# Second block of a two-block transformer: two depthwise-convolution tiles move to ScalarE and GpSimd, two are summed in PSUM, and three more weight blocks are split

## The chip, the cores and the metric

The kernel runs on one core of one Trainium2 chip. The metric is the device time of one execution in microseconds (us). The engines are PE (TensorE, matmuls), DVE (VectorE), ACT (ScalarE), POOL (GpSimd) and SP (SyncE, which issues the loads of weights).

## The reference, cut to what matters

Two transformer blocks run one after the other on 256 tokens of width 1024. The change lies in the second block, whose mixer is half attention (8 heads of 64) and half a gated depthwise convolution over 512 channels with 31 taps:

```python
def conformer_conv(a, g, w_dw, b_dw, ln_g, ln_b):
    u = a * sigmoid(g)
    u = conv_general_dilated(u, w_dw[:, None, :], padding=((30, 0),), feature_group_count=512) + b_dw
    un = (u - mean(u)) * rsqrt(var(u) + 1e-5) * ln_g + ln_b      # over the 512 channels
    return silu(un)

u = rms_norm(h, mix_norm_g)
q, k, v, glu_a, glu_g = split(u @ w_in)
mixed = concat([attention(q, k, v), conformer_conv(glu_a, glu_g, ...)])
h = h + mixed @ w_out
u = rms_norm(h, ffn_norm_g)
h = h + (silu(u @ w_gate) * (u @ w_up)) @ w_down
return rms_norm(h, final_norm_g)
```

## The kernel before, in words

All weights pass through one `Stream` in blocks of 128 partitions x 2048 floats. SP loads a block into one of three raw buffers (`wraw`, L86), so block b waits until block b-3 is done with its buffer. Most blocks are then split: ACT rounds the block to `wh` (L103), DVE subtracts to get the rest `wl` (L104), and PE multiplies with three passes (`mm3`). Three pairs of split buffers rotate in the second block, and a fourth is added for `w_out`. Blocks listed in `NATIVE2` are not split: PE takes the raw fp32 block as it is, and the raw buffer is free only when its matmuls are done.

In the second block `w_in` has ten blocks. Blocks 0 to 3 give the four channel tiles of the convolution (128 channels each, gate and value), 4 and 5 give q, 6 and 7 give k, 8 and 9 give v. `convs` and `proj_cols` are the projections with the result in columns. For each channel tile `ct`, ACT makes the sigmoid `ga`, DVE multiplies to `ug` (L1298), and the convolution is a start (ACT, `cv` = scale times `ug` plus bias, L1310) followed by 30 shifted multiply-adds on DVE, each over 226 to 255 tokens and each on the result of the one before (L1314).

Attention runs in four `STEPS` of four heads by 128 tokens. `scores` makes the logits (PE, `lg`), the row maximum with the bias strip (DVE, `z`, L492), the exponential (ACT, L496), the reciprocal (DVE, L498) and the product with it (ACT, L501); `values` transposes and multiplies with v and splits the result into `oT`. The v projections of blocks 8 and 9 (`proj_tok`, group `pj`) lie behind the scores of steps 0 and 1 and share one PSUM bank, so block 9 waits for the ACT copy of block 8's result. Behind the attention come the layer norm of the convolution (`pmu`, `pvr`, `prs`), its silu, and `w_out` in eight parts of 12 matmuls (`Mix.part`, L196 `acc`), then the feed-forward part.

Each engine takes its instructions in the order in which a scheduler wrote them down when the kernel was built; an instruction that waits holds up all behind it on its engine. `tc.high_priority` and `tc.issue_after` bend that order.

Of the kernel before, what the change touches and what calls it, by code (L numbers as in the profile page):

```python
# [10 lines left out]
F32 = mybir.dt.float32  # L11
# [4 lines left out]
AF = mybir.ActivationFunctionType  # L16
ALU = mybir.AluOpType
AX = mybir.AxisListType

P = 128  # L20
D = 1024
T = 256
# [5 lines left out]
NE = 8  # L28
R_RAW = 3
N_SPLIT = 3  # L30
NATIVE2 = (0, 1, 4, 5, 6, 7)


class Buffers:
# [109 lines left out]
def tile_model(ctx, tc, io, out):  # L144
    nc = tc.nc
# [7 lines left out]
    def ffn_order(w1, w3, w2, n, lag=1):  # L153
        r = []
        for j in range(n):
            r += [w1[j], w3[j]]
            if j >= lag:
                r.append(w2[j - lag])
        return r + [w2[j] for j in range(n - lag, n)]
# [8 lines left out]
    for i in range(len(steps_) + 1):  # L168
        if i < len(steps_):
            e, j = steps_[i]  # L170
            moe_order += [io[n][e][j][kh] for n in ("w1_m", "w3_m") for kh in range(2)]
        if i:
            e, j = steps_[i - 1]
# [5 lines left out]
    order += ffn_order(io["w1_2"], io["w3_2"], io["w2_2"], NF)  # L179
    ws = Stream(tc, rawp, wp, order, native=[second + i for i in NATIVE2])  # L180

# [4 lines left out]
    def bank(group, name):  # L186

        i = groups[group][turns[group] % len(groups[group])]
        turns[group] += 1
        return ps.tile([P, 512], F32, tag="bank%d" % i, name=name)  # L190
# [4 lines left out]
    def mm(o, l, r, start, stop):  # L195
        return nc.tensor.matmul(o, l, r, start=start, stop=stop, skip_group_check=True)  # L196

    def mm3(o, lh, ll, rh, rl, start, stop):
        mm(o, lh, rh, start, False)
        mm(o, lh, rl, False, False)  # L200
        return mm(o, ll, rh, False, stop)
# [5 lines left out]
    def tok(tt):  # L207
        return slice(tt * P, (tt + 1) * P)

    def half(nh):  # L210
        return slice(nh * 512, (nh + 1) * 512)
# [53 lines left out]
    def new_xT():  # L265
        h = xp.tile([P, 8, T], F32R, tag="b8", name="xTh")
        l = xp.tile([P, 8, T], F32R, tag="b8", name="xTl")
        return h, l
# [6 lines left out]
    def take8():  # L275
        return [w if w is None else w.rearrange("p (k n) -> p k n", k=8) for w in ws.take()]
# [4 lines left out]
    def proj_cols(xT, full=None, group="mm"):  # L281

        wh, wl = take8()
        o = bank(group, "pc")
        for ct in range(2):
            for k in range(8):
                oc = o[:, ct * 256:(ct + 1) * 256]
                if wl is None:
                    mm(oc, wh[:, k, tok(ct)], full[:, k, :], k == 0, k == 7)
                else:  # L290
                    mm3(oc, wh[:, k, tok(ct)], wl[:, k, tok(ct)], xT[0][:, k, :], xT[1][:, k, :], k == 0, k == 7)
        return o.rearrange("p (c t) -> p c t", c=2)
# [283 lines left out]
    xT = new_xT()  # L576
# [9 lines left out]
    with tc.tile_pool(name="l0", bufs=1) as lp:  # L586
# [6 lines left out]
        qT = lp.tile([P, 4, T], F32, tag="qT", name="qT")  # L593
        kT = lp.tile([P, 4, T], F32, tag="kT", name="kT")
        vb = lp.tile([P, 2, 512], F32, tag="vb", name="vb")
        with tc.tile_pool(name="gla", bufs=1) as gp:
# [23 lines left out]
            for i in range(2):  # L620
                o = proj_cols(xT)
# [11 lines left out]
            for tt in range(2):  # L633
# [3 lines left out]
                for q in range(2):  # L637
# [5 lines left out]
                    for j in range(2):  # L643
                        rl = g2([P, 2, 256], "rl")
                        nc.scalar.activation(rl[:, :, :S], pis[j][:, :, :S], AF.Relu)
                        for i in range(2):
# [3 lines left out]
                                                           op0=ALU.mult, op1=ALU.add)  # L650
                            first = False
                for r in range(8):
# [4 lines left out]
                                               op0=ALU.not_equal, op1=ALU.max)  # L657
# [76 lines left out]
            for tt in range(2):  # L734
# [13 lines left out]
                for h in range(4):  # L748
                    nc.vector.scalar_tensor_tensor(o_s[:, h, :], o_s[:, h, :], rs[:, h:h + 1], sg[:, tt, tok(h)],
                                                   op0=ALU.mult, op1=ALU.mult)  # L750
# [9 lines left out]
        with tc.tile_pool(name="t0", bufs=1) as tp, tc.tile_pool(name="t0w", bufs=2) as wo:  # L760
# [25 lines left out]
            xT = xT2  # L786
# [3 lines left out]
    with tc.tile_pool(name="f0", bufs=2) as fp, tc.tile_pool(name="f0r", bufs=4) as fr, tc.tile_pool(name="f0w", bufs=1) as fw:  # L790
# [13 lines left out]
        x, xT = xn, xT2  # L804
# [62 lines left out]
    with tc.tile_pool(name="l1", bufs=1) as lp:  # L867
# [6 lines left out]
        with tc.tile_pool(name="fox", bufs=1) as gp:  # L874
# [41 lines left out]
            qT = gp.tile([P, 4, T], F32, tag="qT", name="qT")  # L916
# [30 lines left out]
        with tc.tile_pool(name="t1", bufs=1) as tp, tc.tile_pool(name="t1w", bufs=1) as wo:  # L947
# [5 lines left out]
            copied, logits, xTf = [], [], []  # L953
# [47 lines left out]
    with tc.tile_pool(name="moer", bufs=4) as mr, tc.tile_pool(name="moe2", bufs=2) as m2:  # L1001
# [229 lines left out]
        xT = new_xT()  # L1231
        xTf = xp.tile([P, 8, T], F32, tag="b8", name="xTf")
# [46 lines left out]
    with tc.tile_pool(name="s1", bufs=1) as lp:  # L1279
        def t2(shape, name):  # L1280
            return lp.tile(shape, F32, tag="t2", name=name, bufs=6)

        cw = load_const(lp, "conv_w")
        cpar = load_const(lp, "conv_p")
        strip = load_strip(lp, rows[2])
        c512 = lp.tile([P, P], F32, tag="c512", name="c512")
        nc.gpsimd.memset(c512, 1.0 / 512.0)
        ones = lp.tile([P, P], F32, tag="ones", name="ones")
        nc.gpsimd.memset(ones, 1.0)
        oT = new_oT()  # L1290
        ug = lp.tile([P, 4, T], F32, tag="ug", name="ug")
        ga = lp.tile([P, 4, T], F32, tag="ga", name="ga")
        cv = lp.tile([P, 4, T], F32, tag="cv", name="cv")
        ws.first = True
        for ct in range(4):
            o = convs[ct] if ct < 1 else proj_cols(xT, xTf)
            nc.scalar.activation(ga[:, ct, :], o[:, 0, :], AF.Sigmoid)
            nc.vector.tensor_tensor(ug[:, ct, :], ga[:, ct, :], o[:, 1, :], op=ALU.mult)  # L1298
        qT = lp.tile([P, 4, T], F32, tag="qT", name="qT")
        kT = lp.tile([P, 4, T], F32, tag="kT", name="kT")  # L1300
        for i in range(2):
            nc.scalar.activation(qT[:, 2 * i:2 * i + 2, :], proj_cols(xT, xTf), AF.Copy, scale=0.125)
        for i in range(2):
            nc.scalar.activation(kT[:, 2 * i:2 * i + 2, :], proj_cols(xT, xTf), AF.Copy)
        v = lp.tile([P, 2, 512], F32, tag="v", name="v")
        scores, values = attention(t2, t2, qT, kT, v, lambda h: strip[:, h, :], None, oT, 0, on_act=True)

        def conv(ct):

            nc.scalar.activation(cv[:, ct, :], ug[:, ct, :], AF.Identity, bias=cpar[:, 0, ct:ct + 1],  # L1310
                                 scale=cw[:, ct, 30:31])
            for j in range(30):
                back = 30 - j
                nc.vector.scalar_tensor_tensor(cv[:, ct, back:], ug[:, ct, :T - back], cw[:, ct, j:j + 1],  # L1314
                                               cv[:, ct, back:], op0=ALU.mult, op1=ALU.add)

        for i, step in enumerate(STEPS):
            conv(i)
            scores(*step)
            if i < 2:  # L1320
                nc.scalar.activation(v[:, :, i * 256:(i + 1) * 256], proj_tok(xT, group="pj"), AF.Copy)
            if i:
                values(*STEPS[i - 1])
        with tc.tile_pool(name="t2", bufs=1) as tp, tc.tile_pool(name="t2w", bufs=1) as wo:
            ffng = times32(bcast(tp, io["ffn_g"], "ffng"))
            ws.wider(4, wo, 1)
            xn = xp.tile([P, 2, D], F32, tag="b8", name="h1")
            xT = new_xT()

            def finish(tt, acc):  # L1330
                for nh in range(2):
                    nc.vector.tensor_tensor(xn[:, tt, half(nh)], x[:, tt, half(nh)], acc[nh], op=ALU.add)
                u = tp.tile([P, D], F32, tag="u", name="u", bufs=2)
                rms_tile(xn[:, tt], ffng, u)
                transpose_tile(u, "acc%d" % tt, parts_of(xT, tt))

            mix = Mix(oT, finish)

            pmu = bank("pj", "pmu")
            for ct in range(4):  # L1340
                mm(pmu[:, :T], c512, cv[:, ct, :], ct == 0, ct == 3)
            nc.vector.tensor_tensor(cv, cv, pmu[:, None, :T].to_broadcast([P, 4, T]), op=ALU.subtract)
            nc.scalar.activation(ga, cv, AF.Square)
            values(*STEPS[3])
            mix.part(0, 0)
            pvr = bank("pj", "pvr")
            for tt in range(2):
                for ct in range(4):
                    mm(pvr[:, tt:tt + 1], ga[:, ct, tok(tt)], c512[:, 0:1], ct == 0, ct == 3)
            vr = sp.tile([P, 2], F32, tag="vr", name="vr")  # L1350
            nc.vector.tensor_copy(vr, pvr[:, 0:2])
            rs = rstd_of(vr, 1e-5, n=2)
            mix.part(0, 1)
            dg = lp.tile([P, 2, P], F32, tag="dg", name="dg")
            prs = bank("pj", "prs")
            for tt in range(2):
                nc.vector.tensor_scalar(dg[:, tt, :], ident, rs[:, tt:tt + 1], None, op0=ALU.mult)
                mm(prs[:, tok(tt)], ones, dg[:, tt, :], True, True)
            nc.vector.tensor_tensor(cv, cv, prs[:, None, :T].to_broadcast([P, 4, T]), op=ALU.mult)
            for ct in range(4):  # L1360
                nc.scalar.activation(cv[:, ct, :], cv[:, ct, :], AF.Silu, bias=cpar[:, 2, ct:ct + 1],
                                     scale=cpar[:, 1, ct:ct + 1])
                split_to(oT[0][:, 4 + ct, :], oT[1][:, 4 + ct, :], cv[:, ct, :])
            ws.first = False
            for part in ((1, 0), (1, 1), (0, 2), (0, 3), (1, 2), (1, 3)):
                mix.part(*part)
            x = xn

    with tc.tile_pool(name="f2", bufs=2) as fp, tc.tile_pool(name="f2r", bufs=4) as fr, tc.tile_pool(name="f2w", bufs=1) as fw:
        fing = times32(bcast(fp, io["fin_g"], "fing"))  # L1370

        o = xp.tile([P, 2, D], F32, tag="b8", name="o")
# [158 lines left out]
```

## Time and profile before

| what | value |
|---|---|
| median of 3 runs | 1822.85 us (1820.8 to 1822.95) |
| the profiled execution, its own time | 1823.05 us |
| its span in the trace | 1821.3 us |
| PE, DVE, ACT, POOL busy, share of the span | 97%, 74%, 60%, 5% |

The span is what the trace covers; the 1.75 us around it are part of the measured time. The rows further below are from this one execution. Times in rows are us from the start of the span. A row of a busy time does not tell whether the engine was the one waited for; that is read from the waits and from the order.

### The profile page before, as it was taken

Reading aid. Unit: us, or ns where it says so; the run is one execution under the profiler, and the core shown is the slowest. Engines: PE = TensorE matmul, PEld = TensorE weight load, DVE = VectorE, ACT = ScalarE, POOL = GpSimd, SP = SyncE. Lnnn points to the kernel's source line nnn. Section 1 sums busy time; section 2 is a strip of 40 time slices with the busy share of each in tenths; the row PEclk is TensorE's granted clock in tenths of the full one; section 3 lists DMA queues with packets and bytes.
Section 4 is the critical chain, followed back from the end, with each engine's and each line's share of the span. In section 5 each row is a group of like instructions: output and inputs, shape, how many; then the busy total and the mean of one; then the engine's idle time right before and its main releaser. Section 6 shows DMA issues by size and latency. Waiting matters only on the chain. (4 is left out here: it accounts for less than half of the span.)

```text
span 1821.3 us, 24157 instructions
## 1 busy us (share of the span) xinstructions
PE 1772.5 (97%) x9687; PEld 1495.8 (82%) x9687; DVE 1341.7 (74%) x1370; ACT 1096.1 (60%) x1017; POOL 97.0 (5%) x136
## 2 busy tenths in 40 slices
PE   8999999999999999999999999999999989899998
PEld 7797999888678888888788787887887859789997
DVE  6956544546678888888888888888888978854443
ACT  5454434445567777777777777777777752564332
POOL 1101100010010000000000000000001021010000
PEclk9999999999999999999999999999999999899999
DMA  8453985265489999999999999999999914546530
GB/s 301 162 188 117 394 322 186 70 219 175 148 332 417 370 377 376 373 357 368 381 358 371 383 357 372 377 365 370 372 363 386 397 62 158 203 148 252 187 119 24
DMA packets 75415, 512.45 MB, mean 281 GB/s; under 512 B 8572, under 2 KB 8725, under 8 KB 17312
## 3 DMA queue, kind: packets, MB, share of 16 engines
q1 hardware_dynamic: 66240, 476.15, 69.0%
q0 software_dynamic: 8768, 34.18, 5.0%
q8 instruction: 77, 1.26, 0.3%
q10 hardware_dynamic: 288, 0.52, 0.1%
q14 instruction: 42, 0.34, 0.1%
HBM read 495.57 MB, written 19.96 MB: 283 GB/s over the span
## 5 line engine op out<-in xcount | busy, mean ns | idle before, releaser
L104 DVE TENSOR_TENSOR wl<-wraw,wh 128x2048 fp32r<-128x2048 f32 (+1 forms) x446 | 1012.1, 2287 | 291.7 <-ACT wh L103 290.4
L103 ACT ACTIVATE wh<-wraw 128x2048 fp32r<-128x2048 f32 (+1 forms) x446 | 851.9, 1913 | 458.0 <-issue 128.6
L196 PE MATMUL hh<-wl,eTh 128*128 128x512 f32 x896 | 355.9, 397 | 3.2 <-DVE wl L104 3.2
L196 PE MATMUL hh<-wh,eTh 128*128 128x512 f32 x896 | 355.1, 396 | 0.2 <-ACT eTh L204 0.2
L196 PE MATMUL hh<-wh,eTl 128*128 128x512 f32 x896 | 353.3, 394 | 0.0
L196 PE MATMUL pc<-xTh,wh 128*128 128x256 f32 x944 | 269.4, 285 | 1.4 <-ACT xTh L204 1.4
L196 PE MATMUL pc<-xTl,wh 128*128 128x256 f32 x944 | 268.6, 284 | 1.0 <-DVE xTl L205 1.0
L196 PE MATMUL pc<-xTh,wl 128*128 128x256 f32 x944 | 268.6, 285 | 0.0
L196 PEld LDWEIGHTS hh<-wl,eTh 128*128 128x128 f32 x896 | 168.8, 188 | 45.9 <-DVE wl L104 7.6
L196 PEld LDWEIGHTS hh<-wh,eTh 128*128 128x128 f32 x896 | 168.8, 188 | 39.0 <-ACT eTh L204 0.4
L196 PEld LDWEIGHTS hh<-wh,eTl 128*128 128x128 f32 x896 | 168.8, 188 | 38.0
L196 PEld LDWEIGHTS pc<-xTh,wh 128*128 128x128 f32 x944 | 182.1, 193 | 3.3 <-ACT xTh L204 1.6
L196 PEld LDWEIGHTS pc<-xTl,wh 128*128 128x128 f32 x944 | 182.0, 193 | 2.1 <-DVE xTl L205 1.2
L196 PEld LDWEIGHTS pc<-xTh,wl 128*128 128x128 f32 x944 | 182.2, 193 | 0.4 <-issue 0.2
L196 PE MATMUL acc<-wl,mah 128*128 128x512 f32 x448 | 180.8, 404 | 0.0
L196 PE MATMUL acc<-wh,mal 128*128 128x512 f32 x448 | 176.7, 395 | 0.3 <-DVE mal L205 0.3
L196 PE MATMUL acc<-wh,mah 128*128 128x512 f32 x448 | 163.6, 395 | 0.5 <-ACT mah L204 0.5
L196 PEld LDWEIGHTS acc<-wh,mah 128*128 128x128 f32 x448 | 84.4, 188 | 20.6 <-ACT mah L204 0.9
L196 PEld LDWEIGHTS acc<-wh,mal 128*128 128x128 f32 x448 | 84.6, 189 | 18.4 <-DVE mal L205 0.7
L196 PEld LDWEIGHTS acc<-wl,mah 128*128 128x128 f32 x448 | 84.5, 189 | 17.7
L196 PE MATMUL acc<-wh,ah 128*128 128x512 f32 x176 | 68.7, 391 | 0.0
L196 PE MATMUL acc<-wl,ah 128*128 128x512 f32 x176 | 68.7, 390 | 0.0
(346 smaller groups left out, 1806.2 us busy)
## 6 DMA issues: line engine op xcount, KB each, us to landing
wraw<-in_w_m_dram SPq DMA_DIRECT2D x336, 1024.0 KB, 7.3
wraw<-in_w_d_dram SPq DMA_DIRECT2D x33, 1024.0 KB, 5.9
wraw<-in_w_dram SPq DMA_DIRECT2D x33, 1024.0 KB, 4.8
wraw<-in_w_ab_dram SPq DMA_DIRECT2D x14, 1024.0 KB, 5.2
wraw<-in_w_cd_dram SPq DMA_DIRECT2D x12, 1024.0 KB, 4.9
wraw<-in_w_in_dram SPq DMA_DIRECT2D x10, 1024.0 KB, 4.9
xg_d<-zero POOLq DMA_DIRECT2D x8, 1024.0 KB, 46.4
rows<-scr POOLq DMA_DIRECT2D x3, 1536.0 KB, 12.4
```

The source lines that it names most:

```text
L103: self.last_split = (nc.scalar.activation(wh[:, c], raw[:, c], AF.Copy), nc.vector.tensor_tensor(wl[:, c], raw[:, c], wh[:, c].bitcast(F32 ...
L104: nc.vector.tensor_tensor(wl[:, c], raw[:, c], wh[:, c].bitcast(F32), op=ALU.subtract))
L196: return nc.tensor.matmul(o, l, r, start=start, stop=stop, skip_group_check=True)
```

## The change

Channel tiles 0 and 1 of the convolution leave DVE: for each of the 30 taps ACT writes a scaled, shifted copy of `ug` into one of seven buffers `tap` (L1318), and POOL adds it to `cv` (L1319). Tiles 2 and 3 stay on DVE, but their running sum lies in a PSUM bank (`sums`, taken from group `acc0`) instead of SBUF; the last tap writes to SBUF, and ACT copies the first column (L1325). `NATIVE2` shrinks, so that blocks 5, 6 and 7 are split like the others. (The old tuple's entries count from the second block's first weight block.)

```diff
-NATIVE2 = (0, 1, 4, 5, 6, 7)
+NATIVE2 = (0, 1, 4)
...
+        sums = bank("acc0", "cv")
+        def started(ct):
+            return cv[:, ct, :] if ct < 2 else sums[:, (ct - 2) * T:(ct - 1) * T]
         for ct in range(4):
             o = convs[ct] if ct < 1 else proj_cols(xT, xTf)
             nc.scalar.activation(ga[:, ct, :], o[:, 0, :], AF.Sigmoid)
             nc.vector.tensor_tensor(ug[:, ct, :], ga[:, ct, :], o[:, 1, :], op=ALU.mult)
+            nc.scalar.activation(started(ct), ug[:, ct, :], AF.Identity, bias=cpar[:, 0, ct:ct + 1],
+                                 scale=cw[:, ct, 30:31])
+        def conv(ct, on_pool, between=()):
+            for j in range(30):
+                back = 30 - j
+                if on_pool:
+                    p = lp.tile([P, T], F32, tag="tap", name="tap", bufs=7)
+                    i = len(between) + (j - 30) // 8
+                    with tc.issue_after(between[i].ins) if i >= 0 and between else ExitStack():
+                        nc.scalar.activation(p[:, back:], ug[:, ct, :T - back], AF.Copy, scale=cw[:, ct, j:j + 1])
+                    nc.gpsimd.tensor_tensor(cv[:, ct, back:], cv[:, ct, back:], p[:, back:], op=ALU.add)
+                else:
+                    o = started(ct)
+                    nc.vector.scalar_tensor_tensor((cv[:, ct] if j == 29 else o)[:, back:], ug[:, ct, :T - back],
+                                                   cw[:, ct, j:j + 1], o[:, back:], op0=ALU.mult, op1=ALU.add)
+            if not on_pool:
+                nc.scalar.activation(cv[:, ct, 0:1], o[:, 0:1], AF.Copy)
+        conv(0, True)
-        for i in range(2):
-            nc.scalar.activation(qT[:, 2 * i:2 * i + 2, :], proj_cols(xT, xTf), AF.Copy, scale=0.125)
+        copies = [nc.scalar.activation(qT[:, 2 * i:2 * i + 2, :], proj_cols(xT, xTf), AF.Copy, scale=0.125)
+                  for i in range(2)]
+        conv(1, True, copies)
...
-        def conv(ct):
-            nc.scalar.activation(cv[:, ct, :], ug[:, ct, :], AF.Identity, bias=cpar[:, 0, ct:ct + 1],
-                                 scale=cw[:, ct, 30:31])
-            for j in range(30):
-                back = 30 - j
-                nc.vector.scalar_tensor_tensor(cv[:, ct, back:], ug[:, ct, :T - back], cw[:, ct, j:j + 1],
-                                               cv[:, ct, back:], op0=ALU.mult, op1=ALU.add)
         for i, step in enumerate(STEPS):
-            conv(i)
+            if i < 2:
+                with tc.high_priority():
+                    conv(2 + i, False)
             scores(*step)
```

The order of ACT around the copies of q and k to SBUF (`qT`, `kT`), before: only splits of weight blocks stand between them.

```order
L1302 ACTIVATE qT<-pc 128x512 x2
L103 ACTIVATE wh<-wraw 128x2048
L1304 ACTIVATE kT<-pc 128x512
L103 ACTIVATE wh<-wraw 128x2048
L1304 ACTIVATE kT<-pc 128x512
L103 ACTIVATE wh<-wraw 128x2048
```

The same place of ACT now, from the last taps of tile 1 on (the 128x255 one is the sixtieth of all 60 taps; the split ahead of it is that of block 9).

```order
L1318 ACTIVATE tap<-ug,conv_w 128x252
L103 ACTIVATE wh<-wraw 128x2048
L1318 ACTIVATE tap<-ug,conv_w 128x253
L1318 ACTIVATE tap<-ug,conv_w 128x254
L1318 ACTIVATE tap<-ug,conv_w 128x255
L1334 ACTIVATE kT<-pc 128x512
L103 ACTIVATE wh<-wraw 128x2048
L1325 ACTIVATE cv<-cv 128x1
L1334 ACTIVATE kT<-pc 128x512
```

The first `kT` copy, on which the first logits wait, now stands behind all 60 taps, and each tap from the eighth on waits for the POOL add seven before it.

On DVE, where the second block's work begins, the weight splits and the gate products now come first and in turn (the four `wl` belong to blocks 3, 5, 6 and 7; that of block 2 stands ahead of the piece). The 128x226 to 128x230 rows are the first taps of tile 2.

```order
L1305 TENSOR_TENSOR ug<-ga,pc 128x256
L104 TENSOR_TENSOR wl<-wraw,wh 128x2048
L1305 TENSOR_TENSOR ug<-ga,pc 128x256
L104 TENSOR_TENSOR wl<-wraw,wh 128x2048
L1305 TENSOR_TENSOR ug<-ga,pc 128x256
L104 TENSOR_TENSOR wl<-wraw,wh 128x2048
L1305 TENSOR_TENSOR ug<-ga,pc 128x256
L1322 SCALAR_TENSOR_TENSOR cv<-ug,conv_w,cv 128x226
L1322 SCALAR_TENSOR_TENSOR cv<-ug,conv_w,cv 128x227
L1322 SCALAR_TENSOR_TENSOR cv<-ug,conv_w,cv 128x228
L1322 SCALAR_TENSOR_TENSOR cv<-ug,conv_w,cv 128x229
L1322 SCALAR_TENSOR_TENSOR cv<-ug,conv_w,cv 128x230
L104 TENSOR_TENSOR wl<-wraw,wh 128x2048
```

Tile 2 starts only behind the splits of blocks 3, 5 and 6 and the last gate product; before, the taps of tile 0 followed the first gate product.

On POOL, before, nothing stood between the scaling of `ffng` and the layer norm's rstd (`rs_a`, `rs_b`).

```order
L218 DMA ffng<-in_ffn_g_dram 128x1024
L232 TENSOR_SCALAR ffng<-ffng 128x1024
L365 TENSOR_SCALAR rs_a<-vr 128x2
L367 TENSOR_TENSOR rs_b<-rs_a,mhalf 128x2
```

Now the adds begin ahead of that scaling, which stands behind the third.

```order
L218 DMA ffng<-in_ffn_g_dram 128x1024
L1319 TENSOR_TENSOR cv<-cv,tap 128x226
L1319 TENSOR_TENSOR cv<-cv,tap 128x227
L1319 TENSOR_TENSOR cv<-cv,tap 128x228
L232 TENSOR_SCALAR ffng<-ffng 128x1024
L1319 TENSOR_TENSOR cv<-cv,tap 128x229
```

The other 56 adds follow in one run, each waiting for its tap and, within a tile, for the add before it.

## Rows read from the trace of the kernel before

**Rows 1.** Windows by stage: busy us (x instructions) per engine, granted clock, DMA share, GB/s

```profile
1516.00:1560.00 44.00, 44.00 (x251) 39.88 (x251) 43.22 (x103) 11.17 (x14) 1.63 (x1) 1.00 0.52 181
1560.00:1581.00 21.00, 17.73 (x122) 16.62 (x118) 20.61 (x51) 13.37 (x31) 0.00 (x0) 0.84 0.71 259
1581.00:1603.00 22.00, 18.87 (x115) 14.06 (x113) 9.92 (x33) 15.87 (x39) 0.92 (x2) 0.92 0.14 49
```

**Rows 2.** Chain that ended last: start us, us, what

```profile
1533.58 19.82 DVE cv L1314 x53
...
1572.22 8.59 PE pt L196 x48
...
1602.38 0.60 ACT cv L1361
...
1605.28 10.56 PE acc L196 x45
...
1631.51 5.41 PE pt L196 x44
```

**Rows 3.** Timeline of DVE, convolution: start us, us, what [idle before it]

```profile
1516.45 4.40 DVE L1314 SCALAR_TENSOR_TENSOR cv<-ug,conv_w,cv 128x226 f32<-128x226 f32 x9 [0.67 <-ACT cv L1310]
```

**Rows 4.** Timeline of PE: block 2's first and block 3's last matmul, native blocks, logits

```profile
1520.14 0.47 PE L196 MATMUL pc<-xTh,wh 128*128 128x256 f32 x1
...
1531.72 0.28 PE L196 MATMUL pc<-xTh,wl 128*128 128x256 f32 x1
1531.84 27.79 PE L196 MATMUL pc<-xTf,wraw 128*128 128x256 f32 x128
1559.56 0.71 PE L196 MATMUL lg<-kT,qT 64*128 64x128 f32 x8
...
1622.85 0.28 PE L196 MATMUL pt<-wh,xTh 128*128 128x256 f32 x1
```

**Rows 5.** Timeline of ACT: start, split, copy of v, products with a scale

```profile
1515.82 0.60 ACT L1310 ACTIVATE cv<-ug,conv_p,conv_w 128x256 f32<-128x256 f32 x1 [0.49 <-DVE ug L1298]
1518.68 1.92 ACT L103 ACTIVATE wh<-wraw 128x2048 fp32r<-128x2048 f32 x1 [2.26 <-DMA wraw<-in_w_in_dram]
...
1571.60 0.57 ACT L1321 ACTIVATE v<-pt 128x512 f32<-128x512 f32 x1
...
1591.09 0.90 ACT L501 ACTIVATE z<-z,rsm 128x256 f32<-128x256 f32 x2
```

**Rows 6.** Timeline of POOL, from three stretches

```profile
71.48 3.99 POOL L681 TENSOR_TENSOR sg<-sg,gnorm 128x1024 f32<-128x1024 f32 x1 [24.09 <-ACT sg L679]
...
1513.55 4.08 POOL L232 TENSOR_SCALAR ffng<-ffng 128x1024 f32<-128x1024 f32 x1 [3.21 <-DMA ffng<-in_ffn_g_dram]
...
1617.45 0.19 POOL L363 TENSOR_TENSOR rs_a<-ss,rs_v 128x1 f32<-128x1 f32 x1 [1.21 <-ACT u L399]
1617.72 0.57 POOL L367 TENSOR_TENSOR rs_b<-rs_a,mhalf 128x1 f32<-128x1 f32 x1
1625.66 1.88 POOL L362 TENSOR_SCALAR rs_v<-ss 128x1 f32<-128x1 f32 x1 [7.37 <-ACT u L399]
```

**Rows 7.** Timeline of DVE beside those POOL rows

```profile
70.95 2.29 DVE L104 TENSOR_TENSOR wl<-wraw,wh 128x2048 fp32r<-128x2048 f32 x1 [1.88 <-ACT wh L103]
...
1512.68 2.29 DVE L104 TENSOR_TENSOR wl<-wraw,wh 128x2048 fp32r<-128x2048 f32 x1 [1.11 <-ACT wh L103]
...
1625.18 2.28 DVE L104 TENSOR_TENSOR wl<-wraw,wh 128x2048 fp32r<-128x2048 f32 x1
```

**Rows 8.** Windows, PE alone: length, busy us (x), granted clock, DMA share, GB/s

```profile
1571.00:1578.00 7.00, 5.78 (x27) 0.52 0.70 257
1578.00:1585.00 7.00, 4.91 (x41) 0.99 0.11 46
1585.00:1588.00 3.00, 3.00 (x9) 0.50 0.63 186
```

**Rows 9.** DMA issues: count, KB each, median us from issue to landing

```profile
wraw<-in_w_in_dram SPq DMA_DIRECT2D x7, 1024.0 KB, 4.9
```

## The prediction

> **What bounds the kernel now.** I read the windows by stage first. While the second block projects its first eight weight blocks, PE is never idle (44.00 of 44 us) and DVE almost never (43.22) [rows 1]; in the next two windows PE has 3.3 and 3.1 us of idle time. The chain of waits then tells which of the two sets the end. It runs over DVE's 53 convolution taps, then over the PE matmuls of block 9 from 1572.22 to 1580.81, the silu of the layer norm at 1602.38, the matmuls of `w_out`, and the feed-forward matmuls up to 1636.92 [rows 2]. So the convolution ends (1581) just where the v projection ends. Less DVE work gains only what PE can use, and PE cannot start the logits before the projections are done.
>
> The timeline of DVE gives a tap that waits for the one before it: 4.40/9 = 0.49 us [rows 3]. That of PE gives the cost of a block: blocks 2 and 3, split, take 1520.14 to 1532.00, 5.9 each; the four native ones, blocks 4 to 7, take 27.79, 6.95 each; the logits start at 1559.56 [rows 4].
>
> **Removed and moved.** Sixty taps leave DVE, some 60 x 0.4 = 24 us. Blocks 5 to 7 as split blocks save PE 3 x 1.02 = 3.1, so the projections can end at 1559.56 - 3.1 = 1556.5. DVE pays three `wl` of 2.29 for it (6.9 of the 24 freed), ACT three `wh` of 1.92.
>
> **Added.** On ACT, 60 products with a scale. Two of 128x256 take 0.90, so I take 0.45 each, 27 us in all; a split takes 1.92, a copy of 512 elements 0.57 [rows 5]. ACT had 39.88 of 44 us busy already, but much of that is splits that wait for nothing here. On POOL, 60 adds of about 240 elements, each on the sum before it. No such add is in the trace, so it is bounded from both sides. The 128x1024 product on POOL lies from 71.48 to 75.47 [rows 6], but DVE's `wl`, which also reads two operands from SBUF, runs from 70.95 to 73.24 [rows 7]. If POOL only began at 73.24, it took 2.23 for 1024 elements. That reading has support: the 128x1 `rs_v` at 1625.66, which should be as short as `rs_a` (0.19), took 1.88 and ended at 1627.54, with the `wl` that runs to 1627.46; and `ffng` (4.08 from 1513.55) holds another `wl`, to 1514.97, and 2.66 behind it [rows 6, 7]. So a running `wl` holds POOL. An add is then at least 2.23 x 240/1024 = 0.52 plus the 0.08 between `rs_a` and `rs_b`: 0.60. At most I add the fixed 0.19 of a 128x1 operation: 0.19 + 0.48 + 0.08 = 0.75. I take 0.70, nearer to the upper end, since the 0.19 is paid in every short row.
>
> The Trainium skill, SBUF — State Buffer, section Who interferes with whom, says the same: a VectorE instruction with two SBUF inputs and a GpSimd instruction that reads SBUF exclude each other for the whole instruction, and one SBUF input does not contend. The rows on `rs_v` and `wl` agree (1.88 for 128x1); by that rule the taps summed in PSUM leave GpSimd free, which no row here shows. The Trainium skill, GPSIMD Engine Reference, section Engine selection, speaks against the change: an elementwise operation of two inputs belongs on VectorE, GpSimd being about half as fast. By its add of 2048 elements in 4497 ns, an estimate for 240 is 0.53 and a little, and the sum below would come out near its lower end.
>
> **Where ACT is held.** ACT takes its queue in order, and there are seven `tap` buffers: tap n waits for add n-7. Behind the taps in the same queue stand the splits of blocks 3 and 5 to 9 and, after tap 60, the first `kT` copy. So the logits wait for add 53. I walk through it at 0.70 an add:
> - The start of tile 0 ends at 1516.4 as now [rows 5]; add 1 at 1516.95, add 3 done at 1519.05. `ffng` (2.66) to 1521.7. `wh`(3) stands behind tap 6, and `wl`(3) holds POOL until 1523.1. Add 11 is done at 1528.7.
> - Tap 18, 1529.1; `wh`(5) to 1531.0, `wl`(5) to 1533.3; `wh`(6) to 1534.5, `wl`(6) to 1536.9. POOL does little in between.
> - `wh`(7) stands behind tap 29, but its raw buffer is that of the native block 4, which PE leaves at about 1532.0 + 6.95 = 1538.9; the load lands 4.9 later [rows 9], so the split is 1543.8 to 1545.7, and `wl`(7) holds POOL until 1548.1. The taps up to 29 and their adds are done by then.
> - Adds 29 to 41, 13 x 0.70: 1557.2. Tap 48, `wh`(8) to 1559.5, `wl`(8) to 1561.8. Adds 42 to 50 until 1566.0. Tap 57, `wh`(9) to 1568.4, taps 58 to 60 to 1569.7, `kT` to 1570.2.
>
> The logits thus start at 1570.2, where they now start at 1559.56, and PE idles from 1556.5 on.
>
> **From there to the end of v.** After scores of 0.7, block 8 runs on a PE that has been idle for 14 us. Block 9 before, after less idle time, ran at a granted clock of 0.52, the 1.2 GHz level [rows 8], and took 8.59; I take the same: 1579.5. ACT then makes the split of `w_out` that waits for block 8's buffer (1.92) and the copy of v (0.57): 1582.0. Block 9 at full clock takes 5.9: 1587.9, against 1580.81, which is **+7.1**. PE idles 2.5 us ahead of block 9. Before, the like gap inside 1578 to 1585 (4.91 of 7.00 busy) was followed by 3.00 us at a clock of 0.50 [rows 8], which lose half of that: **+1.5**.
>
> **The tail.** Behind v, 14 taps of tile 3 stand between the attention's short DVE operations, so the silu moves away from the end of v by up to 14 x 0.49 = 6.9; most of it hides in waits that the attention has anyway, and I count 2. But 24 more matmuls of `w_out` (10.56/45 = 0.235 each, 5.6) stand ahead of it in the changed order. What the end gains is at most the PE idle time of 1581 to 1603, 3.1, and the 1.5 of its slow clock, 4.6 in all; at least 0. I take **-3.0**. Sum: 7.1 + 1.5 - 3.0 = +5.6 on the profiled 1823.05 (its span of 1821.3 and 1.75 around it) gives 1828.65; the median is 0.2 below that run, so 1828.4. The changes on DVE cost nothing in this sum: its 24 freed us hide the three `wl` and the later tiles; without that cover tile 3 would end after block 9 and push the silu.
>
> **Rivals.** What a measurement can tell is about 0.2%, 3.65 us.
> - A, the forecast: POOL's adds hold ACT. Add prices of 0.60 and 0.75 put `kT` at 1567.0 and 1572.1, -3.2 and +1.9; with the tail's bounds its own range is 1823.5 to 1833.5. Chance 0.52, of which 0.08 lies within 3.65 of before.
> - B, faster: ACT never waits and the copies of `kT` go out at PE's pace. Logits at 1557, block 8 at full clock to 1563.6, split and copy to 1566.1, block 9 to 1572.0: -8.8, with the tail -11.8: 1811.1. It decides if `kT` leaves before about 1561. Against it: behind `wh`(7) at 1545.7 stand 31 taps, two splits and two copies of q, 13.95 + 3.84 + 1.14, which makes 1564.6 from ACT's rows alone. For it: block 7 may load earlier, or a product be shorter. Chance 0.12.
> - C, no change: POOL is not held by `wl`, or its adds are short, and ACT alone sets `kT`, about 1565. Everything shifts by -5.2: 1823.2. For it: the evidence for the hold is three rows. Chance 0.27, of which 0.04 faster by more than 0.2%.
> - D, slower still: the PSUM-summed taps hold POOL too. They read `ug` and a weight from SBUF. 26 of them stand ahead of the last `wl`; each could cost 0.49, 12.7 at most: 1841. No row of before has such an instruction. Chance 0.09, half of it above 1838.
>
> **The numbers.** Faster 0.12 + 0.04 = 0.16; same 0.23 + 0.08 = 0.31; slower 0.44 + 0.09 = 0.53. The range has to leave out B and half of D: 1818 to 1838; the likeliest case's own is 1823.5 to 1833.5.
>
> **What the profile after would show.** Right: ACT's taps waiting for POOL (tap<-POOL), PE idle by about 10 us or more ahead of the first logits, those at 1567 to 1572, block 8 at half clock, adds of 0.6 to 0.75 that stretch by 2.3 under a `wl`, DVE with idle time. Wrong: logits before 1561 with PE full (B); taps back to back (C); adds that stretch beside PSUM taps (D); or a tail whose PE is still idle after v, by which the -3.0 fails.

## The result and the profile after

The changed kernel takes 1837.88 us (median of 5 runs, 1834.02 to 1841.42) against 1822.95: 1.0085 times as long, with a 95% interval of 1.0068 to 1.0102. It is slower, as forecast, and still inside the range of 1818 to 1838, at its very end; but it is slower by 14.9 us where 5.6 were forecast.

Its profiled execution took 1840.16 us with a span of 1838.4, which is 17.1 more than the span of before (14.9 between the medians: this execution is 2.3 us above the median of its kernel, that of before 0.1). Not all of it need belong to the change. ACT starts the convolution of tile 0 at 1519.72 where it was 1515.82 before [rows 5], although PE, DVE and ACT have the same order of work up to there: it is late by 0.7 us at its first split, which waits for its load, and by 2.9 us already at 68 us of the span; what adds the rest is not shown. In the profiles of the 14 further kernels of this study that start lies between 1514.9 and 1518.8. So I read all that follows from the start of tile 0, called **S** below (1515.82 before, 1519.72 after). From S to the end of the span it is 305.5 us before and 318.7 after: **+13.2**.

The windows of after, two stretches as long as the first two of [rows 1] (columns as there: length, PE, PEld, DVE, ACT, POOL, granted clock, DMA share, GB/s), begin at S:

```profile
1520.00:1564.00 44.00, 40.27 (x293) 38.51 (x291) 19.55 (x26) 30.89 (x59) 38.94 (x42) 1.00 0.54 203
1564.00:1585.00 21.00, 7.34 (x40) 7.14 (x41) 14.54 (x26) 16.87 (x26) 19.51 (x20) 0.52 0.29 101
```

DVE has fallen from 43.22 to 19.55 us, as it should; POOL is now the busy engine (38.94 of 44, then 19.51 of 21); and PE, 17.73 of 21 us busy before, has 7.34 in the second stretch, at the 1.2 GHz level (0.52). Work was taken from an engine that kept up with PE and given to one that does not. The chain of waits shows the link from POOL to PE (start us, us, what):

```profile
1566.84 2.83 POOL cv L1319
...
1577.66 1.22 PE lg L196 x8
1578.89 8.29 PE pt L196 x48
1587.20 1.91 ACT wh L103
1589.65 7.49 PE pt L196 x48
```

An add takes 2.83 when DVE's `wl` of block 8 runs over it:

```profile
1566.83 2.29 DVE L104 TENSOR_TENSOR wl<-wraw,wh 128x2048 fp32r<-128x2048 f32 x1 [7.50 <-ACT wh L103]
```

The logits start at 1577.66, S + 57.9 (S + 43.7 before [rows 4]); block 8 takes 8.29 at the low clock, then the split of `w_out`, then block 9 until 1597.14, S + 77.4 (65.0 before). The timeline of ACT, with the idle time ahead of an instruction and its releaser in brackets, shows how POOL reaches the logits:

```profile
1526.01 1.92 ACT L103 ACTIVATE wh<-wraw 128x2048 fp32r<-128x2048 f32 x1 [3.43 <-DMA wraw<-in_w_in_dram]
...
1552.99 0.49 ACT L1318 ACTIVATE tap<-ug,conv_w 128x228 f32<-128x228 f32 x1 [1.80 <-POOL cv L1319]
...
1559.18 0.49 ACT L1318 ACTIVATE tap<-ug,conv_w 128x236 f32<-128x236 f32 x1 [0.27 <-POOL cv L1319]
...
1564.49 0.50 ACT L1318 ACTIVATE tap<-ug,conv_w 128x243 f32<-128x243 f32 x1 [0.26 <-POOL cv L1319]
...
1576.99 0.57 ACT L1334 ACTIVATE kT<-pc 128x512 f32<-128x512 f32 x1
```

In this stretch, taps 33 (128x228) to 48 (128x243), nearly every tap waits for an add; from one tap to the next it is 0.77 us on average, the pace of POOL, while the product itself takes 0.49 or less. The `kT` copy follows the last tap. Over all 60 taps 30 wait. The list of waits has it in one line (us in total, times, longest):

```profile
ACT tap L1318 <- POOL cv L1319: 12.4, 30, 1.8
```

And POOL's own timeline, where the 57 adds behind the scaling of `ffng` are one row:

```profile
1513.62 0.67 POOL L218 DMA_DIRECT2D conv_w<-in_conv_w_dram  x1 [6.23 <-PE ptr L244]
...
1527.01 58.55 POOL L1319 TENSOR_TENSOR cv<-cv,tap 128x229 f32<-128x229 f32 x57
```

### The profile page after: what moved, and what is told of

It is laid out like the page before. It is cut to its first block, busy times and chain, and to the rows that moved or that the text cites. A ratio compares the mean times of both kernels' runs of the same rounds, so it can differ in the third digit from the quotient of the medians.

```text
span 1838.4 us, 24384 instructions
## 1 busy us (share of the span) xinstructions
PE 1773.2 (96%) x9735; PEld 1498.0 (81%) x9735; DVE 1329.1 (72%) x1313; ACT 1127.4 (61%) x1082; POOL 150.3 (8%) x196
## 5 line engine op out<-in xcount | busy, mean ns | idle before, releaser
L104 DVE TENSOR_TENSOR wl<-wraw,wh 128x2048 fp32r<-128x2048 f32 (+1 forms) x449 | 1020.1, 2289 | 319.7 <-ACT wh L103 317.8
L196 PE MATMUL pc<-xTh,wh 128*128 128x256 f32 x992 | 283.7, 286 | 1.7 <-ACT xTh L204 1.7
L196 PE MATMUL pc<-xTl,wh 128*128 128x256 f32 x992 | 282.5, 285 | 0.8 <-DVE xTl L205 0.8
L196 PE MATMUL pc<-xTh,wl 128*128 128x256 f32 x992 | 282.6, 285 | 0.4 <-DVE wl L104 0.4
L196 PEld LDWEIGHTS pc<-xTh,wh 128*128 128x128 f32 x992 | 191.9, 193 | 3.9 <-ACT xTh L204 2.1
L196 PEld LDWEIGHTS pc<-xTl,wh 128*128 128x128 f32 x992 | 191.7, 193 | 2.0 <-DVE xTl L205 1.1
L196 PEld LDWEIGHTS pc<-xTh,wl 128*128 128x128 f32 x992 | 191.8, 193 | 0.8 <-DVE wl L104 0.6
## 6 DMA issues: line engine op xcount, KB each, us to landing
xg_d<-zero POOLq DMA_DIRECT2D x8, 1024.0 KB, 46.5
```

Source lines behind the costliest of these rows:

```text
L104: nc.vector.tensor_tensor(wl[:, c], raw[:, c], wh[:, c].bitcast(F32), op=ALU.subtract))
```

## The experiments

All times in this table are us behind S, the start of tile 0 in the same profile: the first `kT` copy, the end of the last add, the first silu, the end of the span. The medians are those of the runs; the kernel before had 1822.7 to 1824.0 beside them.

| kernel | kT copy | last add | silu | end | median us | ratio to before, 95% interval |
|---|---|---|---|---|---|---|
| before | 36.9 | none | 86.6 | 305.5 | 1822.95 | 1 |
| changed | 57.3 | 65.8 | 103.2 | 318.7 | 1837.88 | 1.0085, 1.0068 to 1.0102 |
| half_adds | 42.0 | 44.6 | 85.6 | 301.1 | 1821.72 | 0.9994, 0.9985 to 1.0004 |
| kt_first | 46.5 | 70.3 | 100.2 | 314.7 | 1834.08 | 1.0060, 1.0044 to 1.0077 |
| native | 50.2 | 55.4 | 99.0 | 317.5 | 1836.82 | 1.0076, 1.0059 to 1.0092 |
| sbuf_sums | 57.6 | 63.1 | 118.2 | 333.5 | 1852.05 | 1.0158, 1.0141 to 1.0175 |
| pool24 | 39.9 | 61.5 | 99.4 | 315.7 | 1834.66 | 1.0057, 1.0040 to 1.0074 |
| pool19 | 43.5 | 65.1 | 87.7 | 303.2 | 1821.31 | 0.9992, 0.9983 to 1.0002 |
| tail16 | 57.0 | 65.6 | 98.6 | 314.8 | 1836.08 | 1.0067, 1.0051 to 1.0084 |
| split_only | 36.4 | none | 94.3 | 309.1 | 1827.63 | 1.0023, 1.0013 to 1.0032 |
| one_tile | 36.9 | 36.6 | 105.7 | 319.5 | 1836.93 | 1.0069, 1.0052 to 1.0086 |
| one_native | 39.5 | 31.6 | 92.8 | 311.6 | 1830.60 | 1.0040, 1.0025 to 1.0054 |
| pool19_native | 37.0 | 57.1 | 85.2 | 303.8 | 1823.09 | 0.9999, 0.9990 to 1.0009 |
| banks | 57.7 | 66.4 | 112.1 | 329.6 | 1849.12 | 1.0140, 1.0123 to 1.0157 |
| pool19_banks | 43.6 | 67.3 | 100.4 | 317.8 | 1836.61 | 1.0063, 1.0047 to 1.0080 |
| pool19_banks_native | 36.9 | 59.1 | 82.9 | 298.4 | 1816.38 | 0.9955, 0.9939 to 0.9972 |

Edits are against the changed kernel unless said otherwise.

**half_adds: is it the adds that hold ACT?**

```diff
-                    nc.gpsimd.tensor_tensor(cv[:, ct, back:], cv[:, ct, back:], p[:, back:], op=ALU.add)
+                    if j % 2:
+                        nc.gpsimd.tensor_tensor(cv[:, ct, back:], cv[:, ct, back:], p[:, back:], op=ALU.add)
```

> Every second add on POOL is left out, in both tiles, so half of the taps of tiles 0 and 1 never enter the sum; ACT still makes all 60 products. Theory (POOL's adds hold ACT through the seven tap buffers): ACT's 12.4 us of waits on POOL go to under 2, the first kT copy comes 8 to 10 us earlier, 1827 to 1832 us. Rival (ACT's own products and splits set the first kT copy): kT moves by less than 3 us, 1834 to 1838 us.

With half of the adds the `kT` copy comes 15.3 us earlier, more than expected, ACT's waits for POOL fall to 0.9 us, and the time, 1821.7, cannot be told from that of the kernel before. All 60 products are still made. So ACT's own work was not the bound: its 60 products, the splits and the copies of q reach `kT` at S + 42.0, where I had worked out 1564.6, S + 48.8.

**kt_first: does the place of the kT copy alone do it?** The loop over the `kT` copies is put ahead of tile 1's taps:

```diff
+        copies += [nc.scalar.activation(kT[:, 2 * i:2 * i + 2, :], proj_cols(xT, xTf), AF.Copy)
+                   for i in range(2)]
         conv(1, True, copies)
-        for i in range(2):
-            nc.scalar.activation(kT[:, 2 * i:2 * i + 2, :], proj_cols(xT, xTf), AF.Copy)
```

> The two kT copies are written ahead of the taps of tile 1, so on ACT the first stands behind 44 taps in place of 60; nothing else changes. Theory (the order of ACT's queue, with adds of about 0.76 us that hold the taps, makes the logits late): the first kT copy 10 to 13 us earlier than the 1577.0 of the changed kernel, block 8 done by about 1575, but the exponentials still stand behind all 60 taps, so only a part comes back: 1828 to 1833 us. Rival (tile 3's taps on DVE, spread between the attention's operations, set the end): logits earlier, the silu not, 1836 to 1839 us.

`kT` comes 10.8 us earlier, the end only 4.0: the exponentials and the copies of v still stand behind the last taps in ACT's queue, and the first exponential even starts later (S + 64.6, in the changed kernel S + 62.5). An early logit gains little if what follows it waits in the same queue. The time, 1834.1, lies 1.1 us above the theory's range and below the rival's; the silu comes 3.0 us earlier, which the rival had ruled out.

**native: what do the three splits cost?**

```diff
-NATIVE2 = (0, 1, 4)
+NATIVE2 = (0, 1, 4, 5, 6, 7)
```

> Blocks 5, 6 and 7 stay native as before; the convolution is split over the engines as in the changed kernel. Theory (a running wl on DVE holds POOL's adds): three wl of 2.3 us leave POOL's path and three wh leave ACT's queue, so POOL's last add and the first kT copy come about 7 us earlier, and the time is 1829 to 1833 us, since PE's native blocks, 3.1 us longer, hide under the wait for kT. Rival (wl does not hold POOL; 60 adds alone set the pace): the last add moves by less than 2 us, 1835 to 1839 us.

The first half of the theory held: without three `wl` beside them the 57 adds take 47.9 us in place of 58.55, and `kT` comes 7.1 us earlier. The time did not follow: 1836.8, inside the rival's range, for another reason than the rival gave. ACT's list of waits shows what took the place of the hold:

```profile
ACT wh L103 <- DMA wraw<-in_w_out_dram: 8.8, 3, 6.7
```

Splits of `w_out` wait on ACT for their loads, 8.8 us, and the copy of v stands behind them.

**sbuf_sums: who yields when DVE and POOL both read SBUF twice?** The sums of tiles 2 and 3 go back to SBUF, and the bank and ACT's copies of the first column go with that:

```diff
-        sums = bank("acc0", "cv")
...
-            return cv[:, ct, :] if ct < 2 else sums[:, (ct - 2) * T:(ct - 1) * T]
+            return cv[:, ct, :]
```

> The running sums of tiles 2 and 3 lie in SBUF, as before the change, in place of PSUM; the copies of the first column go with that. Theory (a DVE operation with two tensors from SBUF excludes POOL's adds while it runs): the 26 taps of tile 2 that run beside the adds now hold them, 0.49 us each, 6 to 12 us in all, the gap between adds near a DVE tap grows from 0.76 to over 1.0 us, and the time is 1843 to 1850 us. Rival (only long splits hold POOL, or none do): adds keep 0.76 to 0.82 us beside taps, 1835 to 1840 us.

The time is 2 us above the range, and the reason that I gave is wrong: the adds lose next to nothing (median 0.736 us against 0.700, the last one even ends 2.7 us earlier behind S). DVE pays. The first row is from the view of the tile `cv` of sbuf_sums, DVE's taps (min/median/max ns, first and last start); below it stands one stretch of its DVE timeline beside the adds:

```profile
L1321 DVE SCALAR_TENSOR_TENSOR cv<-ug,conv_w,cv x60: 460/876/937, 1539.8 to 1596.4; 128x226 f32<-128x226 f32 x2, 128x227 f32<-128x227 f32 x2, 128x228 f32<-128x228 f32 x2, 128x229 f32<-128x229 f32 x2
```

```profile
1552.48 16.23 DVE L1321 SCALAR_TENSOR_TENSOR cv<-ug,conv_w,cv 128x229 f32<-128x229 f32 x20
```

and the same row of the changed kernel, with its sums in PSUM:

```profile
L1322 DVE SCALAR_TENSOR_TENSOR cv<-ug,conv_w,cv x60: 445/471/488, 1547.1 to 1612.3; 128x226 f32<-128x226 f32 x2, 128x227 f32<-128x227 f32 x2, 128x228 f32<-128x228 f32 x2, 128x229 f32<-128x229 f32 x2
```

20 taps in 16.23 us are 0.81 each, the pace of POOL's adds beside them (about one add for each tap), while the shortest tap takes 0.46: each tap with two tensors from SBUF lets one add go first. With the sum in PSUM no tap is above 0.49. The Trainium skill, SBUF — State Buffer, section Who interferes with whom, has both sides of it: two SBUF inputs on VectorE exclude a GpSimd operation that reads SBUF, one does not; these rows agree (0.876 against 0.471).

The 14 us between the two kernels are not the price of this stretching, though, because the edit changes DVE's order as well. With both sums in one PSUM bank the taps of tile 3 stand behind all of tile 2's; with the sums in SBUF the taps of the two tiles alternate, and 58 of the 60 stand ahead of the first maximum of the logits. That maximum on DVE, in the changed kernel, in sbuf_sums and in banks, a later kernel of this section whose taps alternate too but sum in PSUM:

```profile
1580.08 0.28 DVE L492 CUSTOM_DVE_ANT_0 z<-lg,strip 128x128 f32<-128x128 f32 x1
```

```profile
1595.61 0.28 DVE L492 CUSTOM_DVE_ANT_0 z<-lg,strip 128x128 f32<-128x128 f32 x1
```

```profile
1598.47 0.28 DVE L492 CUSTOM_DVE_ANT_0 z<-lg,strip 128x128 f32<-128x128 f32 x1
```

These are S + 60.4, S + 79.2 and S + 81.6. With a like order the sum in PSUM is worth some 3 us (1849.1 for banks against 1852.1), and the intervals of these two overlap.

**pool24 and pool19: cut the link between adds and ACT.** The tap buffers move to a pool that closes ahead of the feed-forward pools, where memory allows more of them:

```diff
-                    p = lp.tile([P, T], F32, tag="tap", name="tap", bufs=7)
+                    p = tq.tile([P, T], F32, tag="tap", name="tap")
...
+        taps = ExitStack()
+        tq = taps.enter_context(tc.tile_pool(name="taps", bufs=24))
         conv(0, True)
...
+        taps.close()
         with tc.tile_pool(name="t2", bufs=1) as tp, tc.tile_pool(name="t2w", bufs=1) as wo:
```

> The tap buffers lie in a pool of their own that closes ahead of the feed-forward pools, so that there are 24 in place of 7; the order on every engine stays. Theory (POOL's adds hold ACT through the buffers, and through ACT the kT copy): tap n waits for add n-24, so ACT's waits on POOL go from 12.4 us to under 2, the first kT copy comes about 15 us earlier (42 us behind the start of tile 0, as with half of the adds), the last add does not move by more than 3 us, and the time is 1821 to 1827 us. Rival (the buffers are not the link; the length of POOL's run of adds itself holds the end): 1831 to 1838 us although kT comes early.

`kT` comes as early as the theory had it, S + 39.9 (the last add comes earlier too, by 4.3 us, where the theory allowed 3), and yet the time is 1834.7, which is the rival's range. The waits of ACT name the reason, and it is neither theory nor rival:

```profile
ACT wh L103 <- POOL cv L1319: 16.0, 1, 16.0
```

One split of `w_out` waits 16 us for the last add, because its fourth split buffer (`t2w`) now lies where the taps were; the copy of v stands behind it. So the buffer gets memory of its own:

```diff
+        held = ExitStack()
+        wo = held.enter_context(tc.tile_pool(name="t2w", bufs=1))
         taps = ExitStack()
-        tq = taps.enter_context(tc.tile_pool(name="taps", bufs=24))
+        tq = taps.enter_context(tc.tile_pool(name="taps", bufs=19))
...
         taps.close()
-        with tc.tile_pool(name="t2", bufs=1) as tp, tc.tile_pool(name="t2w", bufs=1) as wo:
+        with held, tc.tile_pool(name="t2", bufs=1) as tp:
```

> As the run with 24 tap buffers, but the fourth split buffer of w_out has memory of its own, so that no split of w_out waits for the last add; 19 tap buffers. Theory (POOL's adds hurt only through what waits for them in ACT's queue): kT about 40 us behind the start of tile 0, no wait of a split for POOL, the v copies as early as with half of the adds, 1819 to 1824 us. Rival (the late end of the adds, 60 to 62 us behind that start, or tile 3's taps hold the layer norm): 1827 to 1835 us.

1821.3 us, from 1837.9: inside the theory's range and as fast as the kernel before. POOL's timeline of pool19, with the last 54 of the 60 adds, and below it ACT's waits:

```profile
1521.69 59.49 POOL L1319 TENSOR_TENSOR cv<-cv,tap 128x232 f32<-128x232 f32 x54 [0.15 <-ACT tap L1318]
```

```profile
ACT tap L1318 <- POOL cv L1319: 3.9, 10, 1.3
```

All 60 adds are there, and the last one ends at S + 65.1, as late as in the changed kernel (65.8). But ACT waits for them 3.9 us in place of 12.4. That settles it: the slowness of the adds cost nothing that can be told in itself; what cost was that `kT`, the exponentials and v stood behind taps that waited for adds.

**tail16: what do the late taps of tile 3 cost?**

```diff
-            for j in range(30):
+            for j in range(14 if ct == 3 else 0, 30):
```

> Fourteen of tile 3's thirty taps are left out, so its output is not the reference's; all else as in the changed kernel. Theory (tile 3's taps between the attention's DVE operations push the layer norm and the silu away from the end of v): the silu comes 3 to 5 us earlier behind block 9 (25.8 us in the changed kernel, 21.6 before), 1833 to 1835 us. Rival (the attention's own chain sets the silu and the end): silu within 1 us, 1836.5 to 1839 us.

Behind block 9, which ends at 1591.44 here, the silu comes after 22.1 us in place of 25.8, and the span behind S is 3.9 us shorter, 3.0 of it behind block 9. That is the theory's size for the silu. The time does not decide: the median, 1836.1, fell by 1.8 and lies between the ranges of theory and rival, the intervals of the two kernels overlap, and the profiled execution is the fastest of its four (1831.5 to 1836.7).

**split_only, one_tile, one_native: parts of the change alone.** The first is the kernel before with the new `NATIVE2`; the second sends only tile 0 to POOL; the third is the second with the old `NATIVE2`.

```diff
+        sum1 = bank("acc1", "cv")
...
-            return cv[:, ct, :] if ct < 2 else sums[:, (ct - 2) * T:(ct - 1) * T]
+            return cv[:, ct, :] if ct < 1 else sum1[:, :T] if ct < 2 else sums[:, (ct - 2) * T:(ct - 1) * T]
...
-        conv(1, True, copies)
+        with tc.high_priority():
+            conv(1, False)
```

> The kernel before with blocks 5, 6 and 7 split and nothing else changed. Theory (before, DVE is the limit beside PE: 43.2 of 44 us busy): PE gains 3.1 us that it cannot use, three wl of 2.29 us push the convolution's end 6 us behind block 9, 1825 to 1829 us. Rival (the convolution has room): the 3.1 us of PE come through, 1819 to 1821 us.

1827.6: the theory. `kT` is hardly earlier (S + 36.4 against 36.9), DVE's last tap ends at S + 81.5 (65.3 before), and the silu is 7.7 us later: DVE had no room for three `wl`.

> Only tile 0 goes to ACT and POOL; tile 1 is summed on DVE in a second PSUM bank like tiles 2 and 3. Theory (the harm of the change is the run of 60 adds ahead of kT): with 30 adds POOL is done before the taps can hold kT, logits start at PE's pace, about 41 us behind the start of tile 0, 1818 to 1824 us. Rival (DVE, with 90 taps of 0.48 us and the splits, is late instead): the convolution ends after block 9, 1825 to 1831 us.

The rival's reason, at 5.9 us above its range: `kT` at S + 36.9, as early as before, the adds done at S + 36.6, and 1836.9 us all the same, since DVE's last tap ends at S + 92.4 (65.3 before) and the silu is at S + 105.7.

> Tile 0 alone on ACT and POOL, tiles 1 to 3 summed in PSUM on DVE, blocks 5, 6 and 7 native. Theory (a tap that waits for the one before it costs 0.48 us, two tiles in turn cost 0.38, so 90 taps one tile at a time are as long as 120 in pairs): the convolution ends about when it did before, 1822 to 1827 us. Rival (30 taps fewer are 11 us of DVE that come through): 1816 to 1820 us.

1830.6 is 3.6 us above the theory's range, and the convolution does not end when it did before: DVE's last tap ends at S + 74.1 (65.3 before). 30 taps fewer on DVE did not make its part end sooner. Its first tap starts at S + 13.8 (0.6 before), since tile 0, the first to be projected, is no longer DVE's. ACT, too, waits for the end of a tile there (17.1 us in the copies of the first column, L1326); what that costs was not tried by itself.

**pool19_native, banks, pool19_banks, pool19_banks_native: what is left when the hold is gone?** pool19_native is pool19 with the old `NATIVE2`. The banks kernels give tiles 2 and 3 a PSUM bank each:

```diff
-        sums = bank("acc0", "cv")
+        sums = [bank("acc0", "cv"), bank("acc1", "cv")]
...
-            return cv[:, ct, :] if ct < 2 else sums[:, (ct - 2) * T:(ct - 1) * T]
+            return cv[:, ct, :] if ct < 2 else sums[ct - 2][:, :T]
```

> The same with blocks 5, 6 and 7 native as before the change. Theory: three wl fewer beside the adds, so POOL is done about 10 us earlier, logits at PE's pace, 43 to 44 us behind the start of tile 0, the silu not held, 1817 to 1823 us. Rival (the raw buffers that native blocks hold make the splits of w_out wait for their loads on ACT, as in the native run): 1826 to 1835 us.

1823.1, the upper end of the theory's range, with no difference to pool19 or to before that can be told; the logits start at S + 43.7, as before.

> The changed kernel, but the sums of tiles 2 and 3 lie in a PSUM bank each instead of sharing one; in DVE's order the taps of the two tiles then alternate, and nearly all of them stand ahead of the logits' first maximum. The hold of ACT by the adds stays. Theory (tile 3's late taps were worth 3 to 4 us in the tail): kT as late as in the changed kernel, the silu 20 to 23 us behind block 9 in place of 25.8, 1832 to 1836 us. Rival (with the taps ahead of them, the attention's own DVE work starts later and takes back what the tail gains): 1836 to 1840 us.

> 19 tap buffers and a PSUM bank for each of tiles 2 and 3. Theory (hold of ACT and tile 3's late taps are the two costs of the change, and both are gone): 1815 to 1819 us, below the kernel before. Rival (alternating taps fill DVE while the first logits wait for their maximum): 1820 to 1827 us.

Both theories fell: 1849.1 and 1836.6, far above. The rivals named the reason, at too small a price. In two banks the taps of tiles 2 and 3 alternate, and then DVE's order has nearly all of them, and the splits of blocks 7 to 9 and of `w_out` in between, ahead of the first maximum of the logits. The timelines of DVE of pool19, of pool19_banks and of pool19_banks_native, the first maximum in each:

```profile
1563.20 0.28 DVE L492 CUSTOM_DVE_ANT_0 z<-lg,strip 128x128 f32<-128x128 f32 x1
```

```profile
1584.23 0.28 DVE L492 CUSTOM_DVE_ANT_0 z<-lg,strip 128x128 f32<-128x128 f32 x1
```

```profile
1564.91 0.28 DVE L492 CUSTOM_DVE_ANT_0 z<-lg,strip 128x128 f32<-128x128 f32 x1
```

That is S + 47.2, S + 67.0 and S + 46.2. The `kT` copy comes at the same time in the first two (S + 43.5 and 43.6); the attention starts 20 us later.

> The same with blocks 5, 6 and 7 native. Theory (three wl fewer on DVE, 6.9 us, are worth more than PE's 3.1 us once DVE is full): 1 to 4 us below pool19_banks. Rival (PE sets the start of the logits): 2 to 4 us above it.

With the three blocks native DVE has three `wl` fewer, and all 60 taps stand ahead of the maximum without pushing it: 1816.4 us, below both kernels (0.9955 of before). It is 20.2 us below pool19_banks, far more than the 1 to 4 that I expected, because the two differ in DVE's order, not in 6.9 us of work alone. Whether POOL has a part in the gain over the kernel before is not shown: no run has all four tiles on DVE with their sums in PSUM banks.

## Why the prediction came out as it did

The direction and the mechanism (case A) were right. Two terms of the sum were mis-sized: the 8.6 us (7.1 + 1.5) up to the end of block 9 measured 12.4, and the -3.0 of the tail measured +0.8. SP's timeline has the load of block 7, which the walk to the logits had wrong:

```profile
1539.70 0.33 SPq L86 DMA_DIRECT2D wraw<-in_w_in_dram  x1
```

- **Adds hold ACT, ACT holds kT: shown.** Taking away the buffers' limit (pool19) brought back 16.6 us, half of the adds 16.2. (pool19 also brings POOL's loads forward, as told below; half_adds does not, and gains as much.) The late logits at half clock, block 8 at 8.29 us (8.59 taken), the split and copy of v, block 9 at 7.49 (5.9 + 1.5 taken) all came as worked out.
- **The logits: S + 54.4 forecast (1570.2), S + 57.9 measured; 3.6 us short.** Behind S, tap 18 was done 2.5 us later than worked out, block 7's split began only 0.4 later, and block 8's split was done 3.4 later. Three steps of the walk failed. First, block 3's split was taken as early as before, but it waited 3.43 us for its load: with the tap buffers in `lp`, POOL's loads of `conv_w`, `conv_p` and the strip wait 6.23 us for PE's transposes and are issued 6.1 us ahead of S, not 12.3 as before or 12.4 as in pool19, where the tap buffers lie elsewhere. In pool19 block 3's split waits 0.34. That this load collides with those of the constants is argued from these times, not tried by itself. Second, the walk has ACT wait for block 7's load until S + 28.0; that the split did begin at S + 28.4 is luck, since the load was issued early and the split stood behind taps that waited for adds. Third, with block 7 split the walk has 13 adds to go before tap 48 can start, at 0.70, 9.1 us; the trace has 15 (from tap 33 at 1552.99 to tap 48 at 1564.49), 11.5 us, 0.77 each. The add itself takes 0.70 (median); the 0.08 between two adds, which the price was meant to include, comes on top.
- **The bound on ACT alone was wrong.** I had block 7's load wait for the native block 4. It was issued at 1539.70, when DVE's split of block 5 ended, so the raw buffers do not go round in turn, as I had it where I told the kernel before; and six products in a row took 0.39 us each in the changed kernel (2.35 us from 1520.23), not 0.45. half_adds gives `kT` at S + 42.0 without POOL's hold, not S + 48.8. So rival B's condition (`kT` before about S + 45) could be met, but its price was wrong too: with it met, half_adds and pool19 gained nothing over before that can be told (at most some 3 us by their intervals), not 11.8.
- **The tail: -3.0 forecast, +0.8 measured** (from the end of block 9 to the end of the span 240.5 us before, 241.3 after). The step that failed is that most of tile 3's 14 late taps would hide in the attention's waits: the silu comes 25.8 us behind block 9, 4.2 more than before, where I counted 2, and tail16 brings back 3.0 of the 3.8 behind block 9, by one profiled execution each. The term also took PE's idle time for a gain and put nothing down for work that comes to stand behind block 9: PE's idle time from there to the end of `w_out` did fall, from 3.42 to 1.89 us, but its busy time rose from 31.63 to 34.95, with 16 of the 32 logit matmuls there (3.65 us) in place of 8 (1.82).
- **Rival C** (a running `wl` does not hold POOL) fell: adds under a `wl` take up to 2.8 us, and native made the run of adds 10.7 us shorter. **Rival D** (PSUM taps hold POOL) fell: while 14 of DVE's taps ran (1552.29 to 1559.33) the taps on ACT came 0.77 apart (1552.99 to 1559.18, eight of them), and 0.76 apart behind that, with DVE idle (1559.18 to 1564.49, seven).
- **Outside the sum:** 3.9 us of the profiled difference lie ahead of S. The other kernels' starts spread over 4 us, and this one lies 1.0 us beyond the latest of them, so I take it for the spread of the start; why it is there stays open.

The sum closes: 5.6 + 3.8 (up to the end of block 9, with the clock's part) + 3.8 (tail) = 13.2 behind S, and 3.9 ahead of S make the 17.1 of the two profiled executions.

## What to carry to other kernels

Before work is given to a slow engine, ask not how long that engine takes but who waits for it in order: a producer with few buffers passes the slow engine's pace to all that stands behind it in its queue. More buffers for the handover made the same slow work free; the memory that they take must then not be what the next stage waits for. And a faster order for one chain (kT first, alternate taps) gains only if what comes next in the same queue isn't pushed back by it. Where an edit moves a buffer, compare the order of the engines too before the time is put down to the buffer.

## What the hardware showed that was not expected

When a DVE operation with two SBUF inputs meets a row of POOL adds, it is DVE that is stretched (a tap from 0.46 to a median of 0.88 us in sbuf_sums) and the adds that keep their pace (0.70 to 0.74, medians of the changed kernel and sbuf_sums). With long DVE splits it is mutual: in the changed kernel a `wl` that began well inside an add took 2.53 to 2.81 in place of 2.29, and of the adds one under each `wl` took 2.61 to 2.83 in place of 0.70. A tap that reads its sum from PSUM took 0.47 beside the same adds.
